# A fixed order of the tensor engine in the last attention unit, and a last stage on whole rows of 1024 columns

## The chip, the cores and the metric

The kernel runs on one core of one Trainium2 chip. Its time is the device time of one execution in microseconds (us), the median of several runs. A second source is one profiled execution, from which the trace and its views come. The engines are named PE (tensor engine, with PEld for its weight loads), DVE (vector), ACT (scalar), POOL (GpSimd) and SP (which here only requests transfers); a trailing q (SPq, ACTq) is an engine's own queue of transfer requests.

## What is computed

A decoder block on 512 tokens of 1024 columns with 16 meta tokens in front: an input LayerNorm, ten projections, two attention branches (eight heads of differential attention, sixteen of stick-breaking attention), gates, two branch projections merged by sigmoid gates, an output projection, and a LayerNorm over the residual. Cut to what this case touches:

```python
h = layer_norm(concat(meta, x), emb_ln_g, emb_ln_b)
q_d, k_d, v_d, g_d, q_s, k_s, v_s, g_s, m_d, m_s = split(h @ w_in)
z = q_s @ k_s.T * SB_HEAD_DIM ** -0.5                       # per head and block of queries
log_keep = where(before, log_sigmoid(-z), 0.0)
suffix = cumsum(log_keep, reverse=True) - log_keep
y_s = where(before, exp(log_sigmoid(z) + suffix), 0.0) @ v_s
br_d = (y_d * silu(g_d)) @ w_br_diff
br_s = (y_s * silu(g_s)) @ w_br_sb
merged = sigmoid(m_d + b_gate[0]) * br_d + sigmoid(m_s + b_gate[1]) * br_s
y = merged @ w_out
out = layer_norm(DN_ALPHA * h + y, ln_g, ln_b)[N_META:]
```

## The kernel before

**Precision.** Each float32 operand of a product is split into a rounded high part and the rest, and a product is three matmuls (high by high, high by low, low by high). `hi` casts a weight half on ACT (`wh`, line 183), `lo` takes the rest on DVE (`wl`, line 188). A weight half is 128 rows by four blocks of 128 columns. `prep` (line 192) does both for the half four places ahead (`state["ahead"]`), and asks for further weights with `fetch` (line 134). `wh` and `wl` are two tiles of the pool `w` with six buffers each; the raw weights have a ring of six (`raw`).

**Units.** 16 attention units follow one another: eight heads of the differential branch, then eight pairs of heads of the stick-breaking branch. Beside each unit's attention run projections, so that PE always has large products: for the last unit (u = 15, `last`) these are gate d of pair 7, three merge gates (md 0 to 2) and gate s of pair 7, each 24 matmuls of 512 columns. `run` (line 569) writes both down interleaved: a projection yields its nominal time after each group of three matmuls (0.64), and a list of `steps` with nominal times says when an attention step is written.

**Steps of a stick-breaking unit**, for each of its two heads c: `s_scores` (scores, sigmoids, a scan and a product on DVE into `apad`), three parts of `transposed` (PE transposes `apad` into a PSUM bank; ACT makes the high part `ah`, DVE the rest `al`; part 0 covers 512 columns, part 1 384, part 2 256 and one more block), and `s_values` (a row of matmuls into the bank `av`, the last of them at line 924, then line 928 on ACT copies one half, and in the last unit line 930 on DVE adds it into `ysT`). Nominal times before: the parts at 7.0 + 6.5 c, 0.7 apart, and the values at 10.5 + 6.5 c, in all stick-breaking units alike.

**Who sets the order.** In general a planner does, when the program is built: it simulates the engines, takes what is ready, earlier written first, and gives each engine a fixed sequence. `follow` adds an edge that only orders, and `keep_order` (line 233) strings such edges along what is written from a given place on. Before, this holds for the start of the kernel (line 952) and for everything written behind the units (line 1225, PE, DVE, ACT, POOL and SP). In the units themselves, the last included, the planner is free.

**Behind the units.** The attention's pools are closed and the pool `late` takes their memory: `operands` (casts `gh` on ACT, line 1043, and `gl` on DVE, line 1044), more merge gates (md 3 to 7, ms), whose sigmoid (line 565) writes into `late` too, and then the branch products.

**The last stage.** The output projection for c (two halves of 512 output columns) by t (four tiles of 128 tokens), 24 matmuls each (line 1187), into one of three PSUM banks. The weights `w_out` come as sixteen slices (c, k) of 128 by 512 through the raw ring, and `split_out(c, k)` (lines 1123 and 1124) splits one and then lets `fetch` ask for the next: the slice six places on takes its buffer. Beside the products the residual's input LayerNorm is worked out again from x (`residual`, lines 1158 and 1159: two DVE operations, with gain and bias broadcast over all partitions). Line 1195 adds the product, line 1198 takes statistics; when c = 1 follow their aggregate (line 1203), the reciprocal root on POOL (lines 296 and 297, `frs`), `shift` (line 1208) and `scale` (line 1212) with gain and bias (`lgb`), and two stores of 512 columns. In the last tile the last 256 columns are handled apart, with ACT and POOL helping.

All of it works on half rows, 512 columns: `load_half` loads the halves of gain and bias and of the four tiles of x, each with c = 0 before and c = 1 after the splits (0, 5) to (0, 7). They lie in buffers of `wh` and `wl`. `MEANWHILE` (line 1172) says which residuals and splits are written beside which product.

Of the kernel before, what the change touches and what calls it, by code (L numbers as in the profile page):

```python
# [42 lines left out]


@with_exitstack
def hybrid_block_kernel(ctx: ExitStack, tc: tile.TileContext, x, meta, emb_g, emb_b, w_in, b_gate,
# [128 lines left out]
    def hi(h):  # L175

        assert len(split) == h
        item = items[h]
        assert not second.get(item)
        raw = raw0[:, h // 2, ts(h % 2, 4)] if item is None else sums.pop(h) if isinstance(item, tuple) else raws[item]  # L180
        wh, wl = [wpool.tile([P, 4, P], F32R, tag=w, name=w, bufs=6) for w in ("wh", "wl")]
        split.append((raw, wh, wl))
        s.copy(wh, raw)  # L183
# [397 lines left out]
    with tc.tile_pool(name="att", bufs=1) as ap:  # L581
# [372 lines left out]
        for u, (kind, n) in enumerate(UNITS):  # L954
# [25 lines left out]
            else:  # L980
# [32 lines left out]
                for c in range(2):  # L1013
# [3 lines left out]
                    steps += [(7.0 + 6.5 * c + 0.7 * m, f) for m, f in enumerate(parts)]  # L1017
                    steps.append((10.5 + 6.5 * c, lambda c=c, ta=ta: s_values(unit, c, n, ta)))
# [123 lines left out]
    def half(tag, name):  # L1142
        return wpool.tile([P, 4, P], F32, tag=tag, name=name, bufs=6).rearrange("p a b -> p (a b)")

    vec, hrs = {}, [[None, None] for t in range(NB)]

    def load_half(c):
        tag = ("wh", "wl")[c]
        for name, src in (("eg", emb_g), ("eb", emb_b)):
            vec[name, c] = half({"eg": "wh", "eb": "wl"}[name], name)  # L1150
            nc.sync.dma_start(vec[name, c], src[ts(c, 512)].partition_broadcast(P))
        for t in range(NB):
            hrs[t][c] = half(tag, "hr")
            nc.sync.dma_start(hrs[t][c], x[0, ts(t, P), ts(c, 512)])

    def residual(t, c):
        hr = hrs[t][c]
        v.scalar_tensor_tensor(hr, hr, xmv[:, t, 0:1], vec["eg", c], op0=ALU.subtract, op1=ALU.mult)
        v.scalar_tensor_tensor(hr, hr, xrs[:, t:t + 1], vec["eb", c], op0=ALU.mult, op1=ALU.add)
# [4 lines left out]
    load_half(0)  # L1164
    for k in range(5, KT):
        split_out(0, k)
    load_half(1)
# [4 lines left out]
    MEANWHILE = [[lambda: residual(0, 0)] + [lambda k=k: split_out(1, k) for k in range(3)],  # L1172
                 [lambda: residual(1, 0)] + [lambda k=k: split_out(1, k) for k in range(3, 6)],
                 [lambda: residual(2, 0)] + [lambda k=k: split_out(1, k) for k in range(6, 8)] + [lambda: residual(0, 1)],
                 [lambda: residual(3, 0)] + [lambda t=t: residual(t, 1) for t in range(1, 3)],
                 [lambda: residual(3, 1)], [], [], []]
    for c in range(2):
        for t in range(NB):
            st, final = sts[t], t == NB - 1
            for o, w in [(0, 256), (256, 256)] if final and c else [(0, 512)]:  # L1180
                r, hr = ds(o, w), hrs[t][c]
# [7 lines left out]
                if o == 0:  # L1189
                    for work in MEANWHILE[NB * c + t]:  # L1190
                        work()
                    if t == 0 and c == 0:
# [13 lines left out]
            def shift(c, o, w):  # L1206
                a = hrs[t][c][:, ds(o, w)]
                v.scalar_tensor_tensor(a, a, mv[:, 0:1], lgb[0][:, ds(512 * c + o, w)], op0=ALU.subtract, op1=ALU.mult)

            def scale(c, o, w):  # L1210
                a = hrs[t][c][:, ds(o, w)]
                v.scalar_tensor_tensor(a, a, rs, lgb[1][:, ds(512 * c + o, w)], op0=ALU.mult, op1=ALU.add)  # L1212

            shift(0, 0, 512)
            if final:
                a = hrs[t][1][:, 256:]
                shift(1, 256, 256)
                s.mul(a, a, rs)
                g.tensor_tensor(a, a, lgb[1][:, 768:], op=ALU.add)
            scale(0, 0, 512)  # L1220
            shift(1, 0, 256 if final else 512)
            scale(1, 0, 256 if final else 512)
            for h in range(2):
                nc.sync.dma_start(out[0, ts(t, P), ts(h, 512)], hrs[t][h])
# [30 lines left out]
```

## Time and profile before

| | |
|---|---|
| runs | 714.28 us median of 3 (713.76 to 714.56) |
| the profiled execution | 716.97 us |
| its span, first to last instruction | 714.6 us |
| mean granted clock of PE | 0.993 |
| PE busy | 698.9 us, 98% of the span |
| DVE busy | 571.8 us, 80% |
| ACT busy | 439.1 us, 61% |
| bytes read from HBM, written to it | 91.96 MB, 9.44 MB |

The profiled execution is a little longer than the others because it is recorded; its span is the stretch from the first to the last instruction, and all times inside a trace count from its start. The page divides the span into busy time by engine; a busy PE is not yet a PE at its peak, because the clock that it is granted can fall. The chain of work that ended last is shared out on the page like this: PE 83%, DVE 8%, DMA 4%, ACT 3%.

### The profile page before, as it was taken

The page shows a single profiled execution, that of the slowest core. Times are in us where ns is not written, and L with a number is a line of the kernel's source. Part 1 is how long each engine was busy: PE and PEld are TensorE (multiplying, and loading weights), DVE is VectorE, ACT ScalarE, POOL GpSimd, SP SyncE. Part 2 cuts the span into 40 slices and gives each one's busy share as a digit, 9 for nine tenths or more (in the row PEclk, how much of TensorE's full clock was granted, in tenths as well). Part 3 has the DMA queues.
Part 4 walks back from the last instruction along what each step waited for, and adds up shares of the span by engine and source line. Part 5 has one row for each costly group of instructions (what it writes and reads, how often), then busy time and mean ns, then how long its engine had stood idle before and what let it go on. Part 6 is the DMA issues. An engine that isn't in the chain of part 4 may idle for free.

```text
span 714.6 us, 13390 instructions
## 1 busy us (share of the span) xinstructions
PE 698.9 (98%) x4494; PEld 637.0 (89%) x4494; DVE 571.8 (80%) x1265; ACT 439.1 (61%) x1065; POOL 125.9 (18%) x143
## 2 busy tenths in 40 slices
PE   8999999999999999999999999999989999999994
PEld 7999999989989898998989898888878998999884
DVE  6888898878788678988968989876296788788887
ACT  5776676757667687776848768666265446555300
POOL 3204210212222101212213110000012102130002
PEclk9999999999999999999999999999999999999998
DMA  9358854879987976999799875748249748696902
GB/s 292 95 166 164 177 129 121 185 180 192 191 204 167 225 178 154 192 208 217 197 205 197 203 171 139 199 113 253 79 130 181 150 126 185 136 191 174 321 15 103
DMA packets 182182, 123.36 MB, mean 173 GB/s; under 512 B 9009, under 2 KB 165074, under 8 KB 182114
## 3 DMA queue, kind: packets, MB, share of 16 engines
q1 hardware_dynamic: 148130, 102.32, 50.0%
q0 software_dynamic: 33664, 19.14, 21.4%
q10 hardware_dynamic: 320, 1.06, 0.4%
q8 instruction: 35, 0.57, 0.4%
q14 instruction: 33, 0.27, 0.1%
HBM read 91.96 MB, written 9.44 MB: 142 GB/s over the span
## 4 chain that ended last, share of the span: by engine, by line
PE 83%; DVE 8%; DMA 4%; ACT 3%; issue 1%; POOL 1%; SPq 0%; DVEq 0%; ACTq 0%; POOLq 0%
PE q L690 15%; PE ps L494 11%; PE ps L495 11%; PE ps L496 11%; PE q L1062 10%; PE ps L510 7%; PE sc L754 5%; PE t L766 3%; PE bank L385 1%; PE tv L723 1%; DMA raw<-in_w_in_dram 1%; DMA raw<-in_w_out_dram 1%; DMA lgb<-in_ln_g_dram 1%; DVE hr L1212 1%; DMA xt<-in_x_dram 1%
## 5 line engine op out<-in xcount | busy, mean ns | idle before, releaser
L494 PE MATMUL ps<-hTh,wh 128*128 128x512 f32 x368 | 145.5, 395 | 1.8 <-ACT wh L183 1.8
L188 DVE TENSOR_TENSOR wl<-raw,wh 128x512 fp32r<-128x512 f32 x169 | 115.5, 691 | 38.0 <-ACT wh L183 36.0
L495 PE MATMUL ps<-hTl,wh 128*128 128x512 f32 x368 | 145.3, 395 | 0.0
L496 PE MATMUL ps<-hTh,wl 128*128 128x512 f32 x368 | 145.2, 394 | 0.0
L183 ACT CAST wh<-raw 128x512 fp32r<-128x512 f32 x169 | 104.4, 625 | 30.2 <-PE ps L495 17.3
L494 PEld LDWEIGHTS ps<-hTh,wh 128*128 128x128 f32 x368 | 69.5, 189 | 15.4 <-ACT wh L183 2.2
L496 PEld LDWEIGHTS ps<-hTh,wl 128*128 128x128 f32 x368 | 69.6, 189 | 14.3 <-DVE wl L188 0.4
L495 PEld LDWEIGHTS ps<-hTl,wh 128*128 128x128 f32 x368 | 69.5, 189 | 13.4
L146 POOL DMA_DIRECT2D rawk<-in_w_in_dram x44 | 61.1, 1649 | 95.2 <-DMA rawk<-in_w_in_dram 50.5
L754 PE MATMUL sc<-k,A 128*128 128x264 f32 (+3 forms) x320 | 66.4, 300 | 0.0
L1062 PE MATMUL q<-gh,wh 128*128 128x256 f32 x224 | 63.5, 283 | 0.2 <-ACT t L1071 0.2
L1062 PE MATMUL q<-gl,wh 128*128 128x256 f32 x224 | 63.4, 283 | 0.0
L1062 PE MATMUL q<-gh,wl 128*128 128x256 f32 x224 | 63.4, 283 | 0.0
L907 DVE TENSOR_TENSOR_SCAN e<-e,diag 128x528 f32<-128x528 f32 (+1 forms) x64 | 53.5, 848 | 7.3 <-ACT e L901 7.2
L754 PEld LDWEIGHTS sc<-k,A 128*128 128x128 f32 x320 | 50.5, 189 | 3.2
L690 PE MATMUL q<-tS,wh 128*128 128x264 f32 x176 | 50.9, 290 | 0.9 <-DVE low L612 0.9
L690 PE MATMUL q<-tl,wh 128*128 128x264 f32 x176 | 50.2, 286 | 0.0
L690 PE MATMUL q<-tS,wl 128*128 128x264 f32 x176 | 50.2, 286 | 0.0
L772 DVE TENSOR_TENSOR al<-t,ah 128x512 fp32r<-128x512 f32 (+2 forms) x72 | 39.7, 552 | 12.5 <-ACT ah L771 8.6
L771 ACT CAST ah<-t 128x512 fp32r<-128x512 f32 (+2 forms) x72 | 34.2, 477 | 21.3 <-PE t L766 21.1
L510 PE MATMUL ps<-hTh,wh 128*128 128x264 f32 x160 | 46.4, 290 | 0.2 <-ACT k L632 0.2
L933 POOL DMA_DIRECT2D ys<-half x14 | 11.8, 840 | 196.2 <-ACT ys L932 109.7
(291 smaller groups left out, 1867.0 us busy)
## 6 DMA issues: line engine op xcount, KB each, us to landing
raw<-in_w_in_dram SPq DMA_DIRECT2D x141, 256.0 KB, 3.3
rawk<-in_w_in_dram POOLq DMA_DIRECT2D x44, 256.0 KB, 5.7
rawk<-in_w_in_dram SPq DMA_DIRECT2D x33, 256.0 KB, 3.8
k<-ks SPq DMA_DIRECT2D x60, 132.0 KB, 2.9
raw<-in_w_out_dram SPq DMA_DIRECT2D x16, 256.0 KB, 3.7
k<-ks SPq DMA_DIRECT2D x60, 66.0 KB, 2.6
A<-low SPq DMA_DIRECT2D x28, 128.0 KB, 3.0
raw<-in_w_br_diff_dram SPq DMA_DIRECT2D x12, 256.0 KB, 4.0
```

What stands on the lines that cost most here:

```text
L146: second[l] = [lambda raw=raw, x=x: g.dma_start(raw, x, accum_op=ALU.add) for x in more]
L183: s.copy(wh, raw)
L188: eng.tensor_tensor(wl, raw, wh.bitcast(F32), op=ALU.subtract)
L494: pe.matmul(ps, wh[:, k % 4, :], hTh[:, k, M:], start=(k == 0), stop=False)
L495: pe.matmul(ps, wh[:, k % 4, :], hTl[:, k, M:], start=False, stop=False)
L496: pe.matmul(ps, wl[:, k % 4, :], hTh[:, k, M:], start=False, stop=(k == KT - 1))
L510: pe.matmul(ps[:, :H2], a[:, k % 4, :], b[:, k, ts(c, H2)], start=(k == 0 and m == 0), stop=(k == KT - 1 and m == 2))
L690: pe.matmul(bank, a[:, k, :], b, start=start and k == 0 and j == 0, stop=k == 3 and j == 2, skip_group_check=not start)
L754: pe.matmul(ps[:, :n], q, K[:, m, k0:k0 + n], start=(m == 0), stop=(m == 1))
L772: v.tensor_tensor(l, t[:, o:o + w], h.bitcast(F32), op=ALU.subtract)
L907: v.tensor_tensor_scan(rev, rev, diag[0][:, L - nk:][:, ::-1], 0.0, ALU.mult, ALU.max)
L1062: pe.matmul(bank, a[:, k, :], b[:, n, k, :], start=start and k == 0 and m == 0, stop=k == 3 and m == 2, skip_group_check=not start)
```

## The change

There are two parts.

The last unit gets a list of its own, `LAST`, with the nominal times of the three transposing parts and of the values for each head: later than before for all of them. From the place where the first of them is written, PE's instructions are strung together in the order in which they are written (`state["ends"]`, `keep_order(..., ORDERED[:1])`); the other engines remain the planner's. With a projection yielding 0.64 per group of three matmuls, the list puts the parts of head 0 behind groups 21, 23 and 29 of the last unit's 40, its values behind 34, the parts of head 1 behind 35, 35 and 37, and its values behind 39.

The last stage works on whole rows. `wh` and `wl` become the halves of one tile, `w2` (six buffers), so that one buffer holds 1024 columns. `load_rows(t)` loads the x rows of a tile, and with t = 0 gain and bias too; it is written for t = 0 behind split_out(0, 5) and for the others in `MEANWHILE`. `residual(t)` works on 1024 columns and is written behind the splits of its tile instead of ahead of them. The two `lgb` transfers are written at the third tile instead of the first. `shift` and `scale` work on 1024 columns and one store; in the last tile `scale` and the stores are in two halves, and ACT and POOL no longer take part.

```diff
--- before.py
+++ after.py
@@ -40,7 +40,7 @@
 TD = [(0.85, 11.0, 14.5), (0.95, 13.0, 16.5)]
 GATE_AT = {4: 0, 5: 1, 6: 2, 7: 3, 8: 4, 11: 5, 14: 6}
 LO, HI = slice(0, 64), slice(64, 128)
-
+LAST = [13.0, 14.1, 18.2, 21.2], [21.9, 21.9, 23.2, 24.9]
 
 @with_exitstack
 def hybrid_block_kernel(ctx: ExitStack, tc: tile.TileContext, x, meta, emb_g, emb_b, w_in, b_gate,
@@ -178,7 +178,8 @@
         item = items[h]
         assert not second.get(item)
         raw = raw0[:, h // 2, ts(h % 2, 4)] if item is None else sums.pop(h) if isinstance(item, tuple) else raws[item]
-        wh, wl = [wpool.tile([P, 4, P], F32R, tag=w, name=w, bufs=6) for w in ("wh", "wl")]
+        w2 = wpool.tile([P, 2, 4, P], F32R, tag="w2", name="w2", bufs=6)
+        wh, wl = w2[:, 0], w2[:, 1]
         split.append((raw, wh, wl))
         s.copy(wh, raw)
 
@@ -1014,8 +1015,11 @@
                     ta = {}
                     steps += spread(s_scores(unit, c, n == 0), (2.0 + 4.3 * c) if n == 0 else 4.4 * c, 0.85, 5)
                     parts = transposed(ta, apads[c])
-                    steps += [(7.0 + 6.5 * c + 0.7 * m, f) for m, f in enumerate(parts)]
-                    steps.append((10.5 + 6.5 * c, lambda c=c, ta=ta: s_values(unit, c, n, ta)))
+                    times = LAST[c] if last else [7.0 + 6.5 * c + 0.7 * m for m in range(3)] + [10.5 + 6.5 * c]
+                    steps += zip(times, parts)
+                    steps.append((times[3], lambda c=c, ta=ta: s_values(unit, c, n, ta)))
+                if last:
+                    steps.append((LAST[0][0] - 0.1, lambda: state.update(ends=len(nc.cur_bb.bb.instructions))))
             run(proj, steps)
 
 
@@ -1139,46 +1143,44 @@
         run([pair("BS", p, G, MS[2 * p:2 * p + 2], lambda m, p=p: merged(2 * p + m))], steps)
 
 
-    def half(tag, name):
-        return wpool.tile([P, 4, P], F32, tag=tag, name=name, bufs=6).rearrange("p a b -> p (a b)")
-
-    vec, hrs = {}, [[None, None] for t in range(NB)]
-
-    def load_half(c):
-        tag = ("wh", "wl")[c]
-        for name, src in (("eg", emb_g), ("eb", emb_b)):
-            vec[name, c] = half({"eg": "wh", "eb": "wl"}[name], name)
-            nc.sync.dma_start(vec[name, c], src[ts(c, 512)].partition_broadcast(P))
-        for t in range(NB):
-            hrs[t][c] = half(tag, "hr")
-            nc.sync.dma_start(hrs[t][c], x[0, ts(t, P), ts(c, 512)])
-
-    def residual(t, c):
-        hr = hrs[t][c]
-        v.scalar_tensor_tensor(hr, hr, xmv[:, t, 0:1], vec["eg", c], op0=ALU.subtract, op1=ALU.mult)
-        v.scalar_tensor_tensor(hr, hr, xrs[:, t:t + 1], vec["eb", c], op0=ALU.mult, op1=ALU.add)
+    def whole(name):
+        return wpool.tile([P, 2, 4, P], F32, tag="w2", name=name, bufs=6).rearrange("p a b c -> p (a b c)")
+
+    vec, hrs = {}, []
+
+    def load_rows(t):
+        if t == 0:
+            for name, src in (("eg", emb_g), ("eb", emb_b)):
+                vec[name] = whole(name)
+                nc.sync.dma_start(vec[name], src.partition_broadcast(P))
+        hrs.append(whole("hr"))
+        nc.sync.dma_start(hrs[t], x[0, ts(t, P), :])
+
+    def residual(t):
+        hr = hrs[t]
+        v.scalar_tensor_tensor(hr, hr, xmv[:, t, 0:1], vec["eg"], op0=ALU.subtract, op1=ALU.mult)
+        v.scalar_tensor_tensor(hr, hr, xrs[:, t:t + 1], vec["eb"], op0=ALU.mult, op1=ALU.add)
 
     for _, f in later:
         f()
     later.clear()
-    load_half(0)
     for k in range(5, KT):
         split_out(0, k)
-    load_half(1)
+        if k == 5:
+            load_rows(0)
     WO.append([lp.tile([P, KT, 512], F32R, tag=f"g{x}", name=f"wo1{x}") for x in "hl"])
     lgb = [pair_of("lgb", n=512) for j in range(2)]
     lgb = [t.rearrange("p a b -> p (a b)") for t in lgb]
     sts = [lr.tile([P, 4, 6], F32, tag="fst", name="fst", bufs=4) for t in range(NB)]
-    MEANWHILE = [[lambda: residual(0, 0)] + [lambda k=k: split_out(1, k) for k in range(3)],
-                 [lambda: residual(1, 0)] + [lambda k=k: split_out(1, k) for k in range(3, 6)],
-                 [lambda: residual(2, 0)] + [lambda k=k: split_out(1, k) for k in range(6, 8)] + [lambda: residual(0, 1)],
-                 [lambda: residual(3, 0)] + [lambda t=t: residual(t, 1) for t in range(1, 3)],
-                 [lambda: residual(3, 1)], [], [], []]
+    MEANWHILE = [[lambda k=k: split_out(1, k) for k in range(3)] + [lambda: residual(0), lambda: load_rows(1)],
+                 [lambda k=k: split_out(1, k) for k in range(3, 5)] + [lambda: residual(1), lambda: load_rows(2)],
+                 [lambda k=k: split_out(1, k) for k in range(5, 7)] + [lambda: residual(2), lambda: load_rows(3)],
+                 [lambda: split_out(1, 7), lambda: residual(3)], [], [], [], []]
     for c in range(2):
         for t in range(NB):
             st, final = sts[t], t == NB - 1
             for o, w in [(0, 256), (256, 256)] if final and c else [(0, 512)]:
-                r, hr = ds(o, w), hrs[t][c]
+                r, hr = ds(o, w), hrs[t][:, ts(c, 512)]
                 ps = pj.tile([P, 512], F32, tag="pj", name="pso")[:, :w]
                 products = [(k, m) for k in (0, 1, 2, 3, 4, 5, 7, 6) for m in ("hh", "hl", "lh")]
                 if t == 0 and c == 0:
@@ -1189,7 +1191,7 @@
                 if o == 0:
                     for work in MEANWHILE[NB * c + t]:
                         work()
-                    if t == 0 and c == 0:
+                    if t == 2 and c == 0:
                         nc.scalar.dma_start(lgb[0][:, :], ln_g[0].partition_broadcast(P))
                         nc.scalar.dma_start(lgb[1][:, :], ln_b[0].partition_broadcast(P))
                 v.scalar_tensor_tensor(hr[:, r], hr[:, r], DN_ALPHA, ps, op0=ALU.mult, op1=ALU.add)
@@ -1203,25 +1205,25 @@
             v.bn_aggr(mv, st[:, :4 if final else 2])
             rstd_of(lr, mv[:, 1:2], rs, P)
 
-            def shift(c, o, w):
-                a = hrs[t][c][:, ds(o, w)]
-                v.scalar_tensor_tensor(a, a, mv[:, 0:1], lgb[0][:, ds(512 * c + o, w)], op0=ALU.subtract, op1=ALU.mult)
-
-            def scale(c, o, w):
-                a = hrs[t][c][:, ds(o, w)]
-                v.scalar_tensor_tensor(a, a, rs, lgb[1][:, ds(512 * c + o, w)], op0=ALU.mult, op1=ALU.add)
-
-            shift(0, 0, 512)
-            if final:
-                a = hrs[t][1][:, 256:]
-                shift(1, 256, 256)
-                s.mul(a, a, rs)
-                g.tensor_tensor(a, a, lgb[1][:, 768:], op=ALU.add)
-            scale(0, 0, 512)
-            shift(1, 0, 256 if final else 512)
-            scale(1, 0, 256 if final else 512)
-            for h in range(2):
-                nc.sync.dma_start(out[0, ts(t, P), ts(h, 512)], hrs[t][h])
+            def shift(o, w):
+                a = hrs[t][:, ds(o, w)]
+                v.scalar_tensor_tensor(a, a, mv[:, 0:1], lgb[0][:, ds(o, w)], op0=ALU.subtract, op1=ALU.mult)
+
+            def scale(o, w):
+                a = hrs[t][:, ds(o, w)]
+                v.scalar_tensor_tensor(a, a, rs, lgb[1][:, ds(o, w)], op0=ALU.mult, op1=ALU.add)
+
+            if not final:
+                shift(0, D)
+                scale(0, D)
+                nc.sync.dma_start(out[0, ts(t, P), :], hrs[t])
+                continue
+            shift(0, D)
+            scale(0, 512)
+            nc.sync.dma_start(out[0, ts(t, P), :512], hrs[t][:, :512])
+            scale(512, 512)
+            nc.sync.dma_start(out[0, ts(t, P), 512:], hrs[t][:, 512:])
+    keep_order(state["ends"], ORDERED[:1])
     keep_order(first, ORDERED + [mybir.EngineType.SP])
 
 
```

## The prediction

> **What bounds the kernel now.** I read the page's busy shares first, then the tensor engine's waits, and then only the stretches that held one.
>
> ```profile
> span 714.6 us, 13390 instructions
> PE 698.9 (98%) x4494; PEld 637.0 (89%) x4494; DVE 571.8 (80%) x1265; ACT 439.1 (61%) x1065; POOL 125.9 (18%) x143
> PE ps L494 <- ACT wh L183: 1.8, 1, 1.8
> PE q L690 <- DVE low L612: 0.9, 2, 0.6
> ```
>
> PE is busy for 98% of the span, so the change can win in two ways only: where PE stands still or runs slowly, and in the stretch after its last matmul. PE's longest wait is one of 1.8 us on a weight cast; the next line of importance is 0.9 us in two pieces. The timeline of the engines at that wait (start, length, engine, line, operation, and in brackets what ended the idle time before), and one window behind it (the granted clock is the third number from the end):
>
> ```profile
> 520.96 0.39 PE L496 MATMUL ps<-hTh,wl 128*128 128x512 f32 x1
> 523.17 0.64 PE L494 MATMUL ps<-hTh,wh 128*128 128x512 f32 x1 [1.82 <-ACT wh L183]
> 526.66 0.46 PE L496 MATMUL ps<-hTh,wl 128*128 128x512 f32 x1
> 526.96 0.40 PE L494 MATMUL ps<-hTh,wh 128*128 128x512 f32 x1
> 502.65 0.69 DVE L524 TENSOR_TENSOR sg<-ps,sg 128x512 f32<-128x512 f32 x1
> 517.32 0.58 ACT L928 COPY half<-av 64x512 f32<-64x512 f32 x1 [5.75 <-PE av L924]
> 518.70 0.93 ACT L1043 CAST gh<-ydT 128x256 fp32r<-128x256 f32 x2 [0.81 <-DVE ysT L930]
> 522.51 1.12 ACT L183 CAST wh<-raw 128x512 fp32r<-128x512 f32 x2
> 523.00:526.00 3.00, 2.83 (x7) 2.03 (x8) 2.72 (x6) 2.55 (x6) 0.00 (x0) 0.56 0.23 68
> ```
>
> Read the ACT rows backwards. The cast that PE waits for (522.51) stands behind the casts of the next stage's operands (L1043), which waited for DVE L930, which followed ACT L928, and that had been idle 5.75 us for the last value product of the last unit (L924). That product came 14 us behind the unit's own last projection (gate s, whose result DVE reads at 502.65): the planner had put PE to md products of the next stage in between. The price is more than the wait: from 520.96 to 526.96 ten matmuls start, which at the ordinary 0.227 us apart are 2.27 us and here take 6.00. **3.73 us** are lost, 1.98 before the restart and 1.75 at the granted clock of 0.56 behind it.
>
> The other place is the end:
>
> ```profile
> 649.73 0.39 PE L496 MATMUL ps<-hTh,wl 128*128 128x512 f32 x1
> 650.16 0.69 ACT L565 ACTIVATE ss<-ps,cols 128x512 f32<-128x512 f32 x1 [2.28 <-PE ps L496]
> 704.46 0.28 PE L1187 MATMUL pso<-wo1h,ml 128*128 128x256 f32 x1
> 705.41 0.75 DVE L1212 SCALAR_TENSOR_TENSOR hr<-hr,frs,lgb 128x512 f32<-128x512 f32 x1
> 706.08 0.41 DVE L1195 SCALAR_TENSOR_TENSOR hr<-hr,pso 128x256 f32<-128x256 f32 x1
> 706.87 0.41 DVE L1195 SCALAR_TENSOR_TENSOR hr<-hr,pso 128x256 f32<-128x256 f32 x1
> 707.77 0.26 DVE L1203 BATCH_NORM_AGGREGATE fmv<-fst 128x2 f32<-128x24 f32 x1
> 708.07 1.17 DVE L1208 SCALAR_TENSOR_TENSOR hr<-hr,fmv,lgb 128x512 f32<-128x512 f32 x2
> 708.38 0.87 POOL L297 TENSOR_TENSOR frs<-lne,neghalf 128x1 f32<-128x1 f32 x1
> 709.28 0.75 DVE L1212 SCALAR_TENSOR_TENSOR hr<-hr,frs,lgb 128x512 f32<-128x512 f32 x1
> 710.96 0.48 DVE L1212 SCALAR_TENSOR_TENSOR hr<-hr,frs,lgb 128x256 f32<-128x256 f32 x1
> ```
>
> PE's last matmul ends at 704.74, but DVE takes its result only at 706.87: it is still at work on the tile before. So the end of the last stage is bound by DVE, with PE just in front of it. (An idle reader takes a product 0.04 us after its end, as ACT does at 650.16.)
>
> **The change, part by part.**
>
> *Fixed PE order.* Both value products now stand ahead of the last matmuls of gate s. Nothing is added on PE; the chain L924, L928, L930, L1043 starts some 11 us earlier, so the cast comes while prepared weights still lie ahead of PE. I take the whole 3.73 us. What a fixed order can cost is that PE waits wherever an operand is late:
>
> ```profile
> 509.85 0.49 PE L766 MATMUL t<-ident,apad 128*128 128x128 f32 x3
> 510.84 0.42 DVE L772 TENSOR_TENSOR al<-t,ah 128x256 fp32r<-128x256 f32 x1 [3.60 <-ACT ah L771]
> ```
>
> With DVE free, the last operand (al) is complete 1.41 us after its transposes began (509.85 to 511.26). The new list leaves two groups of three matmuls (1.36 us) between them, and the value product begins with about 0.9 us of other operands. So I cost it at nothing, with 0.9 us of cover; if DVE has other work queued there, PE waits, md products can't step in, and behind PE everything waits.
>
> *One tile for wh and wl.* A cast now waits for the last reader of both halves, one matmul (0.23 us) later than for wh alone.
>
> ```profile
> L183 ACT CAST wh<-raw 128x512 fp32r<-128x512 f32 x169 | 104.4, 625 | 30.2 <-PE ps L495 17.3
> ```
>
> ACT already idles for PE there, and the weights are split four halves ahead of use; it costs nothing, or a shift of the planner's order by some tenths in either direction.
>
> *Whole rows on DVE.*
>
> ```profile
> L1124 DVE TENSOR_TENSOR wo1l<-raw,wo1h 128x512 fp32r<-128x512 f32 x8 | 5.1, 686 | 1.8 <-ACT wo1h L1123 1.8
> L1044 DVE TENSOR_TENSOR gl<-t,gh 128x1024 fp32r<-128x1024 f32 x8 | 9.8, 1225 | 1.5 <-ACT gh L1043 1.5
> 668.52 1.89 DVE L1124 TENSOR_TENSOR wo1l<-raw,wo1h 128x512 fp32r<-128x512 f32 x3
> 670.32 0.68 DVE L1195 SCALAR_TENSOR_TENSOR hr<-hr,pso 128x512 f32<-128x512 f32 x1
> 671.65 0.73 DVE L1158 SCALAR_TENSOR_TENSOR hr<-hr,xmv,eg 128x512 f32<-128x512 f32 x1
> 672.42 0.75 DVE L1159 SCALAR_TENSOR_TENSOR hr<-hr,xrs,eb 128x512 f32<-128x512 f32 x1
> ```
>
> Another 512 columns cost 0.54 us (1225 less 686 ns). L1159 starts 0.77 behind L1158, what follows a pair 0.67 behind its second (705.41 to 706.08): 1.44 a pair, and 2.51 at 1024 columns. One pair for two saves 0.37 us, four times for the residuals and three times for shift and scale, which now also cover some 0.45 us of waiting for frs: about 3.9 us off DVE, more than its backlog. Then the last result is taken 0.04 us behind PE's end, at 704.78: **2.09 us** earlier. From there the shift starts 1.20 later as now, takes 1.31 with 1024 columns (frs, ready 1.18 after the shift's start, is covered), and two scales of 512 add 0.67 and 0.75: 3.93 us to the end of DVE, against 4.57 (706.87 to 711.44): **0.64 us** less. The last store is 128x512 as before. Together 2.73.
>
> *The loads move.* This term takes something back. Gain and bias and the x rows are now requested on SP behind the load that split_out(0,5) sets free:
>
> ```profile
> 660.01 0.42 SPq L1151 DMA_DIRECT2D eg<-in_emb_ln_g_dram  x1
> 664.41 2.95 SPq L144 DMA_DIRECT2D raw<-in_w_out_dram  x3
> 667.06 0.76 DVE L1158 SCALAR_TENSOR_TENSOR hr<-hr,xmv,eg 128x512 f32<-128x512 f32 x1 [1.68 <-DMA hr<-in_x_dram]
> 662.00:664.00 2.00, 2.00 (x11) 1.65 (x10) 1.91 (x4) 1.78 (x4) 0.00 (x0) 1.00 0.89 156
> 664.00:666.50 2.50, 2.50 (x12) 1.79 (x11) 1.38 (x3) 1.97 (x4) 0.00 (x0) 1.00 1.01 285
> 668.00:672.00 4.00, 4.00 (x19) 3.34 (x18) 3.96 (x7) 0.00 (x0) 0.00 (x0) 1.00 1.03 404
> 682.50 0.39 PE L1187 MATMUL pso<-wo1h,mh 128*128 128x512 f32 x1
> ```
>
> So eg goes out at about 664.8 instead of 660.01, and before residual(0) starts 1.05 MB of broadcast gains and biases and 0.52 MB of x must land, twice as much as now. The broadcast's rate is the unknown: 156 GB/s (the last column) while it was eg's and eb's halves, rows of 2 KB; 285 when ln_g and ln_b, rows of 4 KB, joined; 404 in the mixed plateau. Now, from 660.01 to 667.06 are 7.05 us, of which 0.52 MB at 156 and 0.26 MB at 404 explain 4.0: 3.0 us of lead, part of it the neighbour's traffic; without it I estimate 2.0 to 3.0. The ends: 664.8 + 2.0 + 2.6 + 1.3 = 670.7 and 664.8 + 3.0 + 6.7 + 1.3 = 675.8. I take 220 GB/s, between the row of the same operation and that of the same row length, and a lead of 2.5: **673.4**.
>
> What waits for it? DVE's order is fixed: residual(0), L1195 and L1198 of tile 0 (1.33), two splits (1.20), residual(1), 1.33, 1.20, residual(2), 1.33, the last split (0.69): 3 x 2.51 + 3 x 1.33 + 2 x 1.20 + 0.69 = 14.6 us. Then wo1l of k=7 is ready, which PE wants 19 x 0.227 behind 682.50, at 686.8. So residual(0) has to start by 672.2, and each us later is a us of PE. (Tile 0's bank is wanted again 24 matmuls before 682.50; that limit is 673.7.) At 673.4 PE waits **1.2 us**, a gap between the 0.6 and the 1.98 above, and I let the clock stand. The ends: nothing, and 3.6 us. PE's end moves with it; DVE has caught up by then.
>
> The lgb loads, asked for two tiles later, are out of this traffic and are needed some 15 us on.
>
> Sum against this execution: 714.6 - 3.73 - 2.73 + 1.2 = 709.3 of span. The median of 714.28 is 0.3 under the span (the profiled run took 716.97 with what lies around it), so I take 5.26 from the median: **709.0 us**, 0.7% faster. About 0.2% is what a measurement of this kernel can tell from no change.
>
> **The rivals.**
>
> *Early rows* (404 GB/s): residual(0) at 670.7, no wait: 714.28 - 6.46 = 707.8. For it: larger requests, nothing beside them. Against: the 156. The Trainium skill, DMA: Bandwidth & Descriptors, Bandwidth, gives 6.15 us and 341 GB/s for a 1 MB transfer, more for larger ones; by that, an estimate, the rows would be in time, and no row here shows a broadcast alone at such a rate.
>
> *Late rows* (156 GB/s, 675.8): PE waits 2.1 us for the bank and 1.5 for wo1l; the first is like the 1.98 that brought the clock down, so 1.75 more: 714.28 - 6.46 + 5.35 = 713.2.
>
> *The order is fixed but the stall stays*, since something other than the value product holds L1043 or the cast (another buffer of the attention stage). Only the last stage gains: 714.28 - 2.73 + 1.2 = 712.8. Against it: L930 is named as releaser.
>
> *Slower: the fixed order makes PE wait at the value products.* Both need al, and DVE also has the scans of the second half and the weight splits. If DVE's order puts 2.9 us ahead of al at both places, 0.9 are covered and PE stands twice for 2.0, each with 1.75 of slow clock: 709.0 + 7.5 = 716.5. It turns slower than before once both waits exceed 0.9 us with the clock lost (2 x 0.9 + 3.5 against 5.26). For it: the planner put the second product late, so in its reckoning operands were late. Against: DVE idled 3.60 before al.
>
> *The slow clock is not the stall's.* Then 1.98 of the 3.73 goes: 710.8. Against it: the window of 0.56 begins at the restart. The Trainium skill, TensorE: Matmul & The Clock Gate, HAM oscillation, warns of idle gaps above some 3.4 us; by that a 1.8 us gap would keep the clock. The trace decides for the stall.
>
> **How the numbers follow.** Forecast 0.45 (708.2 to 710.4); early rows 0.20; late rows 0.16; stall stays 0.08; slower 0.08; clock 0.03. Below 712.85 (0.2%) fall the forecast, early rows, clock case, half of the late rows and of the stall case: 0.80. Same takes 0.12, slower 0.08. The range goes from 707.4 (early rows, and tenths of the planner's) to 713.0, which holds the late rows but for their end; some 0.17 lie outside.
>
> **What would show it.** Right: no wait of PE on L183 near 520 and a granted clock of 1.00 through 520 to 530; residuals of 1024 columns at 1.28 us; the first residual waiting for x until about 669.7 (673.4 less 3.7), and PE about 1 us for wo1l just behind the start of c=1; the last L1195 directly behind PE's last matmul, and 3.9 us from it to DVE's end. Wrong: a wait of PE on al or av in the last unit; another window near 0.56; a last L1195 still us behind PE; new waits in earlier units, from the merged weight tile.

## The result and the profile after

| | before | after |
|---|---|---|
| median of nine runs each | 714.98 us (713.76 to 716.88) | 712.33 us (711.79 to 713.17) |
| ratio, 95% interval | | 0.9954 (0.9942 to 0.9966) |
| profiled execution, its span | 716.97, 714.6 us | 712.33, 710.5 us |
| first matmul of the last stage | 660.48 | 656.87 |
| last product's result taken by DVE | 706.87 | 702.96 |
| end of DVE | 711.44 | 707.33 |

The kernel became 0.5% faster, 2.65 us between the medians; 5.3 were forecast. The spans differ by 4.1 us, and the two numbers don't contradict each other. The nine runs of before fall into two groups, five of 713.76 to 714.98 and four of 716.60 to 716.88, and the profiled one belongs to the upper. In 17 more runs, where the mean granted clock of each is known, six had 0.995 or 0.996 and took 714.05 to 715.04 us, and eleven had 0.993 or 0.994 and took 715.29 to 717.21. By that, the stall near 520 costs the clock in some executions and not in others; of the kernel before one trace was kept, and there it did. The median for after lies 1.8 us above its span and its profiled run is at the median; so what was said above of the profiled execution, that it is longer because it is recorded, was wrong.

The page after the change, span and busy time by engine:

```profile
span 710.5 us, 13323 instructions
PE 697.8 (98%) x4494; PEld 636.5 (90%) x4494; DVE 569.2 (80%) x1249; ACT 438.5 (62%) x1064; POOL 126.9 (18%) x142
```

PE has as many matmuls as before and is 1.1 us less busy; DVE has 16 instructions fewer. Its longest waits (us in total, times, longest):

```profile
PE warm L307 <- POOL ident masks.py:199: 1.4, 1, 1.4
PE pso L1189 <- DVE wo1l L1128: 0.6, 1, 0.6
PE sc L755 <- DMA k<-ks: 0.6, 1, 0.6
```

The 1.8 us on a weight cast are gone from the list, and a wait of 0.6 us on a split weight of the last stage is new. (The other 0.6 us, of L755 for k, lies in an earlier unit; that line's last matmul starts at 488.4, and the kernel with the fixed order alone doesn't have this wait.) The window behind the place of the old stall (us, then busy time and instructions of PE, PEld, DVE, ACT and POOL, granted clock, DMA share, GB/s):

```profile
520.00:540.00 20.00, 20.00 (x90) 16.57 (x89) 14.24 (x24) 11.25 (x19) 5.28 (x4) 1.00 0.86 176
```

PE is busy for all of the 20 us at a clock of 1.00. The timeline at both places (start, length, engine, line, operation, idle time before it and what ended it):

```profile
504.08 0.39 PE L925 MATMUL av<-al,V 128*128 128x512 f32 x1
504.56 0.58 ACT L929 COPY half<-av 64x512 f32<-64x512 f32 x1 [1.57 <-PE av L925]
506.21 0.93 ACT L1047 CAST gh<-ydT 128x256 fp32r<-128x256 f32 x2
511.26 1.13 ACT L184 CAST w<-raw 128x512 fp32r<-128x512 f32 x2
543.32 0.69 ACT L566 ACTIVATE sm<-ps,cols 128x512 f32<-128x512 f32 x1 [2.59 <-PE ps L497]
656.87 0.40 PE L1189 MATMUL pso<-wo0h,mh 128*128 128x512 f32 x1
660.98 0.42 SPq L1155 DMA_DIRECT2D eg<-in_emb_ln_g_dram  x1
668.75 1.29 DVE L1161 SCALAR_TENSOR_TENSOR hr<-hr,xmv,eg 128x1024 f32<-128x1024 f32 x1 [5.18 <-DMA hr<-in_x_dram]
682.98 0.39 PE L1189 MATMUL pso<-wo1h,mh 128*128 128x512 f32 x1
684.01 0.50 PE L1189 MATMUL pso<-wo1l,mh 128*128 128x512 f32 x1 [0.64 <-DVE wo1l L1128]
701.81 0.28 PE L1189 MATMUL pso<-wo1h,ml 128*128 128x256 f32 x1
702.96 0.41 DVE L1197 SCALAR_TENSOR_TENSOR hr<-hr,pso 128x256 f32<-128x256 f32 x1
704.16 1.31 DVE L1210 SCALAR_TENSOR_TENSOR hr<-hr,fmv,lgb 128x1024 f32<-128x1024 f32 x1
704.47 1.40 POOL L298 TENSOR_TENSOR frs<-lne,neghalf 128x1 f32<-128x1 f32 x1
705.91 1.42 DVE L1214 SCALAR_TENSOR_TENSOR hr<-hr,frs,lgb 128x512 f32<-128x512 f32 x2 [0.44 <-POOL frs L298]
```

Two rows of the kernel before, from the same view of its trace, to set beside them:

```profile
546.92 0.69 ACT L565 ACTIVATE sm<-ps,cols 128x512 f32<-128x512 f32 x1 [2.59 <-PE ps L496]
660.48 0.40 PE L1187 MATMUL pso<-wo0h,mh 128*128 128x512 f32 x1
```

The ledger goes by equal points of the two. The sigmoid of the last merge gate (sm) is 3.60 us earlier, and the first matmul of the last stage 3.61: all that the first part brought is there and stays. PE's last matmul starts 2.65 earlier (704.46 to 701.81), so 0.96 are given back between, most of them at 684.01: that matmul starts 1.03 us behind the one before it instead of 0.227. DVE's end is 4.11 earlier, so behind PE's last matmul 1.46 are won. From its first matmul to DVE's end the last stage takes 50.46 us; before it took 50.96. By these two traces the rewriting of that stage on whole rows is worth 0.50 us in all, and two rows say where the rest went: DVE reads the last product 0.87 us behind its end at 702.09, and it waits 0.44 us for frs, which on POOL takes 1.40 us instead of 0.87.

### The profile page after: what moved, and what is told of

Its sections match the earlier page's. It is cut to its first block, busy times and chain, and to the rows that moved or that the text cites. A ratio compares the mean times of both kernels' runs of the same rounds, so it can differ in the third digit from the quotient of the medians.

```text
span 710.5 us, 13323 instructions
## 1 busy us (share of the span) xinstructions
PE 697.8 (98%) x4494; PEld 636.5 (90%) x4494; DVE 569.2 (80%) x1249; ACT 438.5 (62%) x1064; POOL 126.9 (18%) x142
## 4 chain that ended last, share of the span: by engine, by line
PE 83%; DVE 6%; issue 3%; DMA 3%; ACT 2%; POOL 1%; SPq 0%; POOLq 0%; DVEq 0%; ACTq 0%
PE q L691 15%; PE ps L496 11%; PE ps L497 11%; PE ps L495 11%; PE q L1066 10%; PE ps L511 7%; PE sc L755 5%; PE t L767 3%; PE bank L386 1%; DMA hr<-in_x_dram 1%; PE tv L724 1%; DMA k<-ks 1%; DVE hr L1197 1%; DVE hr L1162 1%; DVE hr L1161 1%
## 5 line engine op out<-in xcount | busy, mean ns | idle before, releaser
L189 DVE TENSOR_TENSOR w<-raw,w 128x512 fp32r<-128x512 f32 x169 | 114.7, 685 | 40.3 <-ACT w L184 37.7
L495 PE MATMUL ps<-hTh,w 128*128 128x512 f32 x368 | 145.0, 394 | 0.0
L497 PE MATMUL ps<-hTh,w 128*128 128x512 f32 x368 | 144.6, 393 | 0.0
L496 PE MATMUL ps<-hTl,w 128*128 128x512 f32 x368 | 144.3, 392 | 0.0
L184 ACT CAST w<-raw 128x512 fp32r<-128x512 f32 x169 | 104.1, 626 | 18.0 <-PE ps L497 7.7
L1066 PE MATMUL q<-gh,w 128*128 128x256 f32 x448 | 81.4, 283 | 0.2 <-ACT t L1075 0.2
L497 PEld LDWEIGHTS ps<-hTh,w 128*128 128x128 f32 x368 | 69.2, 188 | 13.8
L496 PEld LDWEIGHTS ps<-hTl,w 128*128 128x128 f32 x368 | 69.2, 188 | 13.0
L495 PEld LDWEIGHTS ps<-hTh,w 128*128 128x128 f32 x368 | 69.2, 188 | 12.9
L691 PE MATMUL q<-tS,w 128*128 128x264 f32 x352 | 75.1, 290 | 0.0
L1066 PEld LDWEIGHTS q<-gh,w 128*128 128x128 f32 x448 | 70.1, 192 | 0.5 <-ACT t L1075 0.4
L755 PE MATMUL sc<-k,A 128*128 128x264 f32 (+3 forms) x320 | 66.6, 297 | 0.9 <-DMA k<-ks 0.6
L511 PE MATMUL ps<-hTh,w 128*128 128x264 f32 x320 | 64.4, 288 | 0.2 <-ACT k L633 0.2
L755 PEld LDWEIGHTS sc<-k,A 128*128 128x128 f32 x320 | 50.3, 188 | 3.9 <-ACT e L902 0.8
L511 PEld LDWEIGHTS ps<-hTh,w 128*128 128x128 f32 x320 | 51.4, 189 | 0.6 <-ACT k L633 0.4
```

What stands on the lines that cost most here:

```text
L189: eng.tensor_tensor(wl, raw, wh.bitcast(F32), op=ALU.subtract)
L495: pe.matmul(ps, wh[:, k % 4, :], hTh[:, k, M:], start=(k == 0), stop=False)
L496: pe.matmul(ps, wh[:, k % 4, :], hTl[:, k, M:], start=False, stop=False)
L497: pe.matmul(ps, wl[:, k % 4, :], hTh[:, k, M:], start=False, stop=(k == KT - 1))
L511: pe.matmul(ps[:, :H2], a[:, k % 4, :], b[:, k, ts(c, H2)], start=(k == 0 and m == 0), stop=(k == KT - 1 and m == 2))
L691: pe.matmul(bank, a[:, k, :], b, start=start and k == 0 and j == 0, stop=k == 3 and j == 2, skip_group_check=not start)
```

## The experiments

The theory after this result: the fixed order brings the gain; the whole rows bring little, since their rows of x arrive late (which leaves DVE a backlog to the end) and since the long shift holds back frs. The rivals: the gain or the loss comes from the merged weight tile; the end is as it is because whole rows are no cheaper on DVE; the lgb transfers, asked for two tiles later, matter. Times are compared with runs of before on the same chip: 715.91 us, median of 17, beside the first four kernels, and 715.76, median of 14, beside the other three.

**The fixed order alone, on the kernel before** (two weight tiles, half rows as before).

```diff
+LAST = [13.0, 14.1, 18.2, 21.2], [21.9, 21.9, 23.2, 24.9]
...
-                    steps += [(7.0 + 6.5 * c + 0.7 * m, f) for m, f in enumerate(parts)]
-                    steps.append((10.5 + 6.5 * c, lambda c=c, ta=ta: s_values(unit, c, n, ta)))
+                    times = LAST[c] if last else [7.0 + 6.5 * c + 0.7 * m for m in range(3)] + [10.5 + 6.5 * c]
+                    steps += zip(times, parts)
+                    steps.append((times[3], lambda c=c, ta=ta: s_values(unit, c, n, ta)))
...
+    keep_order(state["ends"], ORDERED[:1])
```

> Only the fixed order of PE in the last unit, the last stage as before. Theory: the 1.8 us wait of PE near 520 and the stretch at half clock behind it are the fixed order's, worth 3.6 us at the end of the projections; the last stage then runs as before, so the span should be near 714.6 - 3.6 = 711.0, with about 7.0 us from PE's last matmul's start to DVE's end, and the first matmul of the last stage near 656.9. Rival: part of the 3.6 us comes from the merged weight tile, which lets the planner order the units differently; then the wait near 520 goes but the last stage starts later than 658. As to the two groups of times of the kernel before (714 and 716.7): if they are the half clock behind the wait, which depends on where the wait falls, the runs of this kernel lie within about 1 us.

Measured: 711.88 us (711.42 to 712.54), ratio 0.9939 (0.9926 to 0.9951), span 710.1. The stall near 520 is gone. The last stage begins at 656.39, and residual(0) starts 6.30 us behind that (6.58 before). DVE in the last tile, timeline:

```profile
702.40 0.40 DVE L1199 SCALAR_TENSOR_TENSOR hr<-hr,pso 128x256 f32<-128x256 f32 x1
703.60 1.17 DVE L1212 SCALAR_TENSOR_TENSOR hr<-hr,fmv,lgb 128x512 f32<-128x512 f32 x2
706.50 0.48 DVE L1216 SCALAR_TENSOR_TENSOR hr<-hr,frs,lgb 128x256 f32<-128x256 f32 x1
```

From the last product to DVE's end are 4.58 us (702.40 to 706.98), against 4.57 before: the tail of half rows is untouched, and the whole time is yet that of the changed kernel, or a little less. So the first part alone explains the result, and the merged tile is not needed for it. The stage takes 50.59 us (656.39 to 706.98), 0.37 less than before with the same code. PE takes the same time in both (43.96 and 43.98 us from the first matmul to the last), and DVE reads the last product 1.77 us behind its end instead of 2.13; that residual(0) starts 0.28 us earlier goes with it, and why it does isn't shown. So against this trace the whole rows gain 0.13 us in the stage, and as they were built they aren't shown to be worth anything beside the fixed order. Of the fixed order itself the later nominal times and the strung sequence were not tried apart.

**The whole rows alone** (the changed kernel with the old nominal times and without the order of the last unit).

```diff
-                    times = LAST[c] if last else [7.0 + 6.5 * c + 0.7 * m for m in range(3)] + [10.5 + 6.5 * c]
-                    steps += zip(times, parts)
-                    steps.append((times[3], lambda c=c, ta=ta: s_values(unit, c, n, ta)))
+                    steps += [(7.0 + 6.5 * c + 0.7 * m, f) for m, f in enumerate(parts)]
+                    steps.append((10.5 + 6.5 * c, lambda c=c, ta=ta: s_values(unit, c, n, ta)))
...
-    keep_order(state["ends"], ORDERED[:1])
```

> Only the whole rows (with the merged weight tile and the moved loads), PE's order in the last unit left to the planner. Theory: the 1.8 us wait near 520 stays, with the half clock behind it; the last stage gains 1.46 us behind PE's end and gives 0.95 back where PE waits for wo1l: span near 714.6 - 0.5 = 714.1, ratio to before 0.998 to 1.0. Rival: the merged tile alone brings the values forward and most of the gain; then the wait near 520 is gone here too and the span is near 711. If the two groups of times of the kernel before come from the half clock behind the wait, the times of this kernel spread over 2 us as well.

Measured: 716.66 us (714.94 to 717.69, 12 runs), ratio 1.0010 (0.9998 to 1.0021). The stall is there, longer than before; the timeline at its end:

```profile
523.85 0.80 PE L495 MATMUL ps<-hTh,w 128*128 128x512 f32 x1 [2.72 <-ACT w L184]
```

And the window behind it:

```profile
524.00:527.00 3.00, 3.00 (x7) 2.25 (x8) 2.69 (x6) 2.23 (x5) 0.00 (x0) 0.50 0.36 106
```

Seven matmuls in 3 us at a clock of 0.50. The last stage takes 50.34 us (661.07 to 711.41), and PE waits 0.53 for wo1l. The chain to the late cast is the same as before, but all of it comes 0.68 us later (its L929 copies at 505.50 and 518.00, against 504.81 and 517.32 of L928 before); two waits of PE for k, 0.26 and 0.37 us, lie ahead of it, and before has none. Whether the merged tile has a part in that isn't shown. So the second part by itself makes no difference that can be measured, and the two parts don't need each other: order alone 0.9939, both 0.9954, rows alone 1.0010.

**The shift in two pieces of 512** (from the changed kernel, in all tiles). It tells whether frs is long because of what runs on DVE beside it.

```diff
-                shift(0, D)
+                shift(0, 512)
+                shift(512, 512)
```

> The changed kernel with shift in two operations of 512 columns instead of one of 1024, in all four tiles; scale as it is. Theory: POOL's power (frs) cannot end until about 0.4 us after the DVE operation that runs when it starts, and so the whole-row shift delays it from 0.88 to 1.40 us and leaves DVE waiting 0.44 us in each tile. Then frs takes about 0.88 us here, scale follows the second shift without a wait, a tile takes about 4.35 us of DVE instead of 4.65, the last L1197 comes 0.04 to 0.3 us behind PE's end instead of 0.87, and the span falls by 0.9 to 1.2 us to about 709.4. Rival: frs is slower for another reason (its own operands, its place in POOL's queue): then its 1.40 us and the waits stay, and the extra operation costs 0.14 us a tile: span 710.6 to 711.

Measured: 711.76 us (710.54 to 711.97), ratio 0.9932 (0.9920 to 0.9945), span 709.7. The tail, timeline of DVE and POOL:

```profile
702.57 0.40 DVE L1197 SCALAR_TENSOR_TENSOR hr<-hr,pso 128x256 f32<-128x256 f32 x1
703.76 1.44 DVE L1210 SCALAR_TENSOR_TENSOR hr<-hr,fmv,lgb 128x512 f32<-128x512 f32 x2
704.07 0.87 POOL L298 TENSOR_TENSOR frs<-lne,neghalf 128x1 f32<-128x1 f32 x1
705.12 1.40 DVE L1214 SCALAR_TENSOR_TENSOR hr<-hr,frs,lgb 128x512 f32<-128x512 f32 x2
```

An operation more on DVE, and the stage is shorter: 49.15 us (657.37 to 706.52) against 50.46. frs takes 0.87, DVE waits for it no longer but in the first tile (0.46 us there), and from the last product to DVE's end are 3.95 us, near the 3.93 of the prediction. As each tile now takes DVE less time (4.44 us from shift to shift instead of 4.65), its backlog at the last product shrinks too, from 0.87 to 0.32 us behind PE's end at 702.25. Of the 1.31 us these are 0.97; the other 0.34 lie on PE, whose wait for wo1l was 0.33 us, as the first residual started 0.32 us earlier in this trace; the edit comes later and has no part in that. So the duration of frs is set by the DVE operation beside it. In the whole time the intervals of this kernel and of the changed one still touch.

**The rows asked for earlier** (from the changed kernel): the loads of gain, bias and the first rows of x go out ahead of the splits (0, 5) to (0, 7) instead of behind the first of them.

```diff
+    load_rows(0)
     for k in range(5, KT):
         split_out(0, k)
-        if k == 5:
-            load_rows(0)
```

> The changed kernel with load_rows(0) ahead of the splits (0, 5) to (0, 7) instead of behind the first, so the first rows are requested some 4 us earlier. Theory: the first residual then starts before 667, DVE has the last split ready in time, PE's wait of 0.64 us for wo1l (0.95 us of start to start) goes, and DVE, ahead by some 3 us, has caught up by the last tile, so the 0.87 us between PE's end and the last L1197 go too: span near 710.5 - 1.8 = 708.7. Rival 1: the loads land no earlier, since the broadcast is slow or the engines are busy with the weights: nothing changes. Rival 2: DVE's lateness at the end is made by the waits for frs alone and not by its late start: only 0.95 goes, 709.6, and the last L1197 still comes 0.8 us late.

Measured: 710.98 us (709.92 to 711.88, six runs), ratio 0.9923 (0.9910 to 0.9936), span 708.2. The requests, the first residual and the tail in the timeline:

```profile
655.84 0.42 SPq L1155 DMA_DIRECT2D eg<-in_emb_ln_g_dram  x1
663.45 1.29 DVE L1161 SCALAR_TENSOR_TENSOR hr<-hr,xmv,eg 128x1024 f32<-128x1024 f32 x1 [0.45 <-DMA hr<-in_x_dram]
700.60 0.42 DVE L1196 SCALAR_TENSOR_TENSOR hr<-hr,pso 128x256 f32<-128x256 f32 x1 [0.23 <-PE pso L1188]
703.56 1.41 DVE L1213 SCALAR_TENSOR_TENSOR hr<-hr,frs,lgb 128x512 f32<-128x512 f32 x2 [0.44 <-POOL frs L298]
```

The first residual starts 7.14 us behind the stage's first matmul (656.31) instead of 11.88, PE's wait for wo1l is gone, and the last product is taken 0.04 us behind its end: now DVE waits for PE, as the prediction had it. The stage takes 48.66 us (to 704.97), 1.80 less than with the changed kernel: 0.97 on PE and 0.83 of backlog. The wait of 0.44 for frs is unchanged; from the last product to DVE's end are still 4.37.

**Both** (rows early and the shift in two pieces).

> The two amendments together: load_rows(0) ahead of the splits, and shift in two operations of 512 columns. From the traces of each alone the last stage takes 49.15 us (two shifts) and 48.66 (rows early) from its first matmul to DVE's end, against 50.46 in the changed kernel and 50.96 before. Theory: with early rows DVE is no longer behind at the end, so of the 0.3 us a tile that two shifts save only the last tile's counts: about 48.3 to 48.4, ratio to before about 0.992. Rival: the two gains add (1.31 and 1.80): 47.4.

Measured: 710.35 us (709.67 to 711.76, six runs), ratio 0.9929 (0.9913 to 0.9944), span 708.2. The tail in the timeline of DVE:

```profile
701.05 0.42 DVE L1196 SCALAR_TENSOR_TENSOR hr<-hr,pso 128x256 f32<-128x256 f32 x1 [0.43 <-PE pso L1188]
703.63 1.40 DVE L1213 SCALAR_TENSOR_TENSOR hr<-hr,frs,lgb 128x512 f32<-128x512 f32 x2
```

The stage takes 48.31 us (656.72 to 705.03), 0.35 less than with early rows alone; from the last product to the end are 3.98 instead of 4.37, and that wait is gone. The two gains don't add up (1.80 and 1.31 by themselves, 2.15 together), because the backlog that shorter tiles take away is the one that early rows take away. The times with early rows, in one piece or two, can't be told apart; the two kernels are the fastest of the study.

**The changed kernel once more**, beside the last one and the next.

> The changed kernel again, beside the others. The order alone gave 0.9939 and the whole rows alone 1.001; if the two parts do not act on one another the whole change is 0.994 to 0.995, the same as the order alone within the interval. With no long wait of PE its runs should have a clock of 0.995 to 0.998 and lie within 1.5 us, while the kernel before again falls into a group near 714.6 at 0.996 and one near 716.5 at 0.993.

Measured: 712.56 us (712.21 to 712.91), ratio 0.9957 (0.9944 to 0.9970); stage 50.52 us (657.41 to 707.93), first residual 11.96 behind its start, wait for wo1l 0.68. The result and its ledger repeat, and the slowest of the six runs above (711.76) is faster than the fastest of these.

**The lgb transfers at the first tile again.**

```diff
-                    if t == 2 and c == 0:
+                    if t == 0 and c == 0:
                         nc.scalar.dma_start(lgb[0][:, :], ln_g[0].partition_broadcast(P))
```

> The changed kernel with the two lgb transfers written at the first tile again, as before the change. Theory: they then share the engines with the first gain, bias and x rows, and the first residual, which starts 11.88 us behind the last stage's first matmul, starts 1 to 2 us later; PE's wait for wo1l grows from 0.64 us by as much, and the span with it: 711.5 to 712.5. Rival: the broadcast of gain and bias is limited by itself and not by its neighbours; then the first residual starts as in the changed kernel, and nothing changes.

Measured: 713.21 us (712.77 to 713.63, seven runs), ratio 0.9964 (0.9952 to 0.9975). In the timeline:

```profile
669.65 1.28 DVE L1161 SCALAR_TENSOR_TENSOR hr<-hr,xmv,eg 128x1024 f32<-128x1024 f32 x1 [6.15 <-DMA hr<-in_x_dram]
684.90 0.50 PE L1189 MATMUL pso<-wo1l,mh 128*128 128x512 f32 x1 [1.61 <-DVE wo1l L1128]
```

The first residual starts 12.85 us behind the stage's start (656.80), about 0.9 later, and PE waits 1.61 for wo1l, 0.9 to 1.0 longer. The stage takes 51.41. This small edit of the change is worth 0.9 us of the stage, just under what was expected. The two broadcasts do move while the rows are awaited: from 660 to 666 the transfer engines carry 352 GB/s and are busy throughout (share 1.01), where the changed kernel has 209 and 0.68.

## Why the prediction was off in size and right in kind

The time fell inside the range and the sign was right; the likeliest value was 3.3 us too low, and the 708.2 to 710.4 of the forecast itself don't hold the measured 712.33. That the range does is in part luck: it had been drawn out to 713.0 for late rows, which didn't come. By its own steps:

- **Fixed PE order: 3.73 us.** Right, for the profiled execution. 3.61 us are gone at the first matmul of the last stage, there is no wait near 520 and the clock is 1.00. The rival of a wait at the value products shows nowhere: L925 at 504.08 follows its neighbours at once, and PE's only listed wait on al is one of 0.2 us in the whole trace (a transpose, L767). The order alone gives 0.9939.
- **One tile for two: nothing.** Not contradicted: in the changed kernel no new wait on a weight cast stands among PE's longest. But with the whole rows alone the wait on the cast was 2.72 us instead of 1.82, the tile wasn't tried by itself, and a small cost of it stays open.
- **Whole rows: 2.73 us.** This step failed by half: 1.46. Two of its sentences were wrong. "frs, ready 1.18 after the shift's start, is covered": frs was taken at the duration that it has beside an operation of 512 columns, but beside one of 1024 it takes 1.40 instead of 0.87, so that it ends some 0.40 us behind that shift too and can't be covered by it. In two pieces the shift gives a tail of 3.95, as forecast. And "DVE has caught up by then": with that wait in each tile, a tile of c = 1 takes DVE 4.65 us (694.56 to 699.21 from shift to shift) instead of 5.03 before (697.71 to 702.74), 0.38 less and not 0.82, while the first residual starts 5.3 us later behind the stage's start than before; 0.83 us of backlog were left. Early rows take exactly that away. The two shifts of before:

```profile
697.71 0.78 DVE L1208 SCALAR_TENSOR_TENSOR hr<-hr,fmv,lgb 128x512 f32<-128x512 f32 x1
702.74 0.78 DVE L1208 SCALAR_TENSOR_TENSOR hr<-hr,fmv,lgb 128x512 f32<-128x512 f32 x1
```

- **The loads move: 1.2 us.** Right, 0.96. The request went out 4.11 us behind the stage's first matmul where 4.3 was forecast (664.8 less 660.48), and the rows were there 7.77 us after it (660.98 to 668.75) against 8.6. DVE's chain from residual(0) to the last split took 15.2 us instead of 14.6, and PE waited 0.64 and started 0.80 late. The clock didn't fall.
- **From the span to the median: 714.28 less 5.26.** This was the largest error, some 2.1 us. The 5.26 came from an execution of 716.97 us that had lost the clock behind the stall; the median of three from which they were taken came from executions that took 2.7 us less. The row that could have warned was in the table: 716.97 beside 713.76 to 714.56. For those three the stall most likely cost 1.98 and not 3.73 (their clock is not known), or the base was 716.97, from which 709.3 of span plus 2.4 would have been 711.7.

The sum of spans was 709.3 and 710.5 was measured: 1.27 too little at the tail, 0.24 too much for the loads, 0.12 of the stall. Of the rivals, the stall that stays (712.8) and late rows (713.2) give times nearer to the measured one than the forecast, but neither is what happened: the stall is gone, the bank was not waited for, and the clock was not lost. Early rows is half confirmed: asked for at the head of the queue, rows arrive in time, and the end that the prediction drew, DVE behind PE by 0.04 us, comes about.

## What to carry to other kernels

A cost of a clock that is lost only sometimes belongs to some executions: look at which group the profiled run is in before its microseconds are taken from a median. When an operation is made longer to cover a small one on another engine, ask whether the small one can run beside it at all; two pieces can end before one does. A load that is "just behind" another in a queue of requests waits for the buffer that the other waits for: whether it stands ahead or behind cost more here (4.7 us in the arrival, 1.8 in the end) than the size of its rows (at the same place in the queue the first residual started 7.14 us behind the stage's start with whole rows and 6.58 with half rows).

## What the hardware showed that was not expected

**POOL waits for DVE.** The same operation on 128 single numbers, frs, has three durations. The changed kernel, first tile of c = 1 and the next, timeline of DVE and POOL:

```profile
689.65 1.29 DVE L1210 SCALAR_TENSOR_TENSOR hr<-hr,fmv,lgb 128x1024 f32<-128x1024 f32 x1
689.70 1.29 POOL L297 TENSOR_TENSOR lne<-fmv,epsr 128x1 f32<-128x1 f32 x1 [43.92 <-DVE fmv L1205]
691.07 0.57 POOL L298 TENSOR_TENSOR frs<-lne,neghalf 128x1 f32<-128x1 f32 x1
694.56 1.31 DVE L1210 SCALAR_TENSOR_TENSOR hr<-hr,fmv,lgb 128x1024 f32<-128x1024 f32 x1
694.60 0.19 POOL L297 TENSOR_TENSOR lne<-fmv,epsr 128x1 f32<-128x1 f32 x1 [2.97 <-DVE fmv L1205]
694.88 1.41 POOL L298 TENSOR_TENSOR frs<-lne,neghalf 128x1 f32<-128x1 f32 x1
699.21 1.31 DVE L1210 SCALAR_TENSOR_TENSOR hr<-hr,fmv,lgb 128x1024 f32<-128x1024 f32 x1
```

And the kernel with the fixed order alone:

```profile
698.28 0.78 DVE L1212 SCALAR_TENSOR_TENSOR hr<-hr,fmv,lgb 128x512 f32<-128x512 f32 x1
698.59 0.87 POOL L298 TENSOR_TENSOR frs<-lne,neghalf 128x1 f32<-128x1 f32 x1
```

At 691.07 the shift is over and DVE idle: 0.57 us. Beside a shift of 512 columns it takes 0.87 and ends 0.40 us behind the shift's end (699.46 and 699.06); beside one of 1024 it takes 1.41 and ends 0.42 behind (696.29 and 695.87). So it doesn't seem to run more slowly, but to stand until the shift is done. Its forerunner on POOL, lne, does the same in the first tile: it takes 0.19 us in the others, and there 1.29, to 0.05 us behind the shift's end. The Trainium skill, SBUF — State Buffer, section "SBUF: two separate sides", gives a rule of this kind: a DVE operation with two operands in SBUF and a GpSimd operation that reads SBUF exclude each other for the whole instruction. The runs agree with it for frs: the shift reads hr and lgb, and halving it took 0.53 us off frs (1.40 to 0.87). But in the later tiles lne ran in 0.19 us while the shift was under way (694.60 to 694.79); what lets it pass there, no run here shows.

**A short stall can cost the clock, and where it falls seems to decide.** Before the change, with PE's gap of 1.8 us near 520, the mean clock of the run was 0.993 or 0.994 in 19 of 31 runs and 0.995 or 0.996 in 12; the medians of the two are 716.41 and 715.01 us. With a gap of 2.7 us (whole rows alone) the mean was as low in 9 of 12 (0.992 or 0.993), and with one of 1.6 us (lgb at the first tile) in none of 7. The Trainium skill, TensorE: Matmul & The Clock Gate, HAM oscillation, speaks of gaps above some 3.4 us; here shorter ones were enough. The Trainium skill, on the same page, What's actually happening, calls the window in which activity is counted free-running.

The traces say more. The half clock lasts 3.41 us in both that show it (523.37 to 526.78 before, 523.76 to 527.17 with the whole rows alone). The kernel before loses the clock once more behind its last matmul, at 707.69, 184.32 us after the first time, which is 54 times 3.413. So I cut each trace into such stretches, counted back from its last loss. PE was busy for 1.60 us of the stretch ahead of the loss at 523.37, 0.79 and 1.52 ahead of the two losses with the whole rows alone, and 1.50 ahead of the one at the end with rows early. Of the stretches behind which the clock stayed, PE was busy least in those with 1.78 us (700.90 to 704.31, the changed kernel once more), 1.80 (682.03 to 685.44, lgb at the first tile, with the whole wait of 1.61 us in it) and 2.14 (698.49 to 701.90, the order alone). In these traces the clock is thus lost behind a stretch of which PE is busy for less than about half. By that a wait of 1.8 us costs the clock if it lies whole in one stretch and may not if it is split between two, and one of 1.6 us doesn't. Where the stretches begin differs from trace to trace; for the executions without a trace it isn't known, so that this explains the 19 of 31 is likely and not shown.
